# Room for two units of query weights, scalings on VectorE, spread splits and a later place for the value products

## The chip, the cores and the metric

The kernel runs on one core of one Trainium2 chip, as one program. The metric is device time in microseconds; the time before is the median of three runs, 2215.27 us (2212.75 to 2215.79). TensorE is called PE here, VectorE DVE, ScalarE ACT, GpSimd POOL, and SP is the engine that issues most DMA transfers.

## The reference

One inference step of an encoder with two layers, model width 1024, on 1024 prompt frames and 32 sample frames. Layer 0 is a recurrent mixer with a matrix memory (8 heads, chunks of 64), followed by a SwiGLU feed-forward part of width 2816. Layer 1 is windowed attention with 16 query heads and 2 shared key/value heads of 64, a learned sink per head and a linear distance bias, followed by another such feed-forward part. After each of the four parts the residual stream goes through `LayerNorm(alpha * x + part(x))`. The change lies in the attention:

```
q = x @ w_q;  k, v = split(x @ w_kv)
s = q k^T / 8 + bias                          # own chunk of 64 and the two chunks before
mx = max(max(s), sink)
p = exp(s - mx) / (sum exp(s - mx) + exp(sink - mx))
mix = (p v) @ w_out
x = LayerNorm(alpha * x + mix)
```

All values are 32-bit floats.

## The kernel before

**Numbers in two parts.** PE multiplies 32-bit floats of a rounded kind. Each operand is therefore split into a high part (a rounded copy) and a low part (operand minus high part), and each product is made of three matmuls: high by high, high by low, low by high. That is `gemm` (L416 to L418), in which nearly all matmuls of the program stand. Activations lie transposed, 128 features by 1056 columns for each of eight tiles k: `ACT` in full, `SX` as high and low part. Columns are cut into three groups (384, 384, 288) in the projections and into four quarters of 264 in the norms and the output projection.

**Weights.** The class `Weights` brings weights in units of 128 by 1024, in the fixed order in which they are used. A unit is loaded into one of four raw buffers (L168, on the SP queue; the load of a unit waits for the buffer of the unit four before) and split in two halves, or seven combinations for the feed-forward products. A split is a copy to the high part (L245 on ACT, or L243 on POOL for chosen halves) and a subtraction for the low part (L247, mostly on POOL). The results go to one of `SLOTS` = 5 slots. A half that has an entry in `W.home` goes to that place instead and needs no slot. `_next` makes the next split of the order or refuses: all slots in use, or the home still in use. Since the order is fixed, a refused half holds up all that follow it. `feed` calls it once per `W.pause` of issued matmul time; `done` frees the slots of a unit.

**Order of the work.** The program is written out as instruction streams, one per engine, each run in order. `Weave` mixes the work: side tasks are generators that yield how many microseconds of matmuls are to be issued before their next step, and each step of a `gemm` ticks them. So the order in which ACT, DVE and POOL get their work follows the matmuls of the issue order, not real time.

**From layer 0 to layer 1.** The last feed-forward products of layer 0 end with norms of the four quarters (`ln_task`, L477 to L531; DVE centres and scales, ACT squares, applies gain and bias and makes the high part at L525, DVE or POOL the low part at L531). While the last two norms run, the key unit and the value unit (`keys_values(0)`) and the first four query units (`q_group`, evacuated at L1686 by ACT and at L1689 by DVE) are multiplied for the first column group. Then the last norms are issued to their end, new PSUM pools are opened and the two score banks `psS` get columns cleared by DVE (L1752). The tasks `v_turn` (transposes the values, L1772, into `VR`) and `attention` are launched, and `keys_values(1)` and `keys_values(2)` follow with the next key unit and value unit. Until then the tiles for keys (`KH`, `KL`, two each of 1184 columns) beyond column 384 and for values (`VR`, 2560 columns) are allocated and empty.

**The attention** is a pipeline of six stages over items (head pair j, block b): `scores` (PE L1817, bias and maximum on DVE L1823), `soft` (ACT L1838), `scale` (reciprocal on DVE L1848, multiplication by it on POOL: L1851 for blocks of two chunks, L1855, one instruction per part, for the first and the last block), `turn` (PE transposes L1876, high part ACT L1880, low part DVE L1881), `values` (PE L1905, into the one bank `O`), `place` (ACT L1919 and DVE L1923 bring the result into `ACT`). A pass over the stages follows the last argument of `pipeline`, the tuple of stage numbers; a stage with a pause lets matmuls of the projections be issued before the next one.

**Splits of outputs.** The attention's output is split into `SX` for the output projection by `mixed_parts` (ACT L446, DVE or POOL L447), column group by column group and tile by tile: eight tiles k of a group need the query projections of that group to be done (`free`) and the tile's items to be placed (`mixed`). After each four tiles of the later groups, a DMA on SP brings the residual back (L1227). `nparts` counts finished groups and is what the output projection waits for. When the first quarter of the output projection is issued, `finish` issues what is left of the attention and of the splits at once.

Of the kernel before, what the change touches and what calls it, by code (L numbers as in the profile page):

```python
# [17 lines left out]
D = 1024  # L18
KT = D // P
# [12 lines left out]
EARLY = 3  # L32
# [18 lines left out]
FEED_W = 1.7  # L51
# [15 lines left out]
GRP = ((0, 384), (384, 384), (768, 288))  # L67
# [223 lines left out]
def kernel(ctx: ExitStack, tc: tile.TileContext, A, O):  # L291
    nc = tc.nc
# [61 lines left out]
    U_KV, U_QB, U_OUT_B = [], [[], []], [[], []]  # L354
# [857 lines left out]

    def mixed_parts(src, free, mixed, pauses, low=(nc.vector,)):


        for g in range(3):
            t0, n = GRP[g]
            while not free(g):
                yield 0.3
            for k in range(KT):  # L1220
                while not mixed(k, g):
                    yield 0.3
                split_act(k, g, low[k % len(low)])
                if g == 0:
                    nc.sync.dma_start(act[k][g], src[:, k, t0 : t0 + n])
                elif k % 4 == 3:
                    nc.sync.dma_start(act_g[g][:, k - 3 : k + 1], src[:, k - 3 : k + 1, t0 : t0 + n])  # L1227
                yield pauses[g]
            nparts[0] += 1

# [398 lines left out]
    home = [pb.tile([P, D // 2], F32R, name=f"oh{i}")[:] for i in range(2)]  # L1629
    W.home.update({(u, 1): home for u in U_QB[0][0:4:2] + U_OUT_B[0][:EARLY] + U_OUT_B[0][EARLY + 1 :: 2]})  # L1630
    vT = act[KT - 1]
# [95 lines left out]
    def keys_values(g):  # L1727
        if g == 2:
            k_part(ck[:], SEQ, P)
        for f, w in ((k_group, U_KV[g > 0][0]), (v_group, U_KV[g > 0][1])):  # L1730
            f(g)
            if g != 1:
                W.done(w)

    for t in tasks[:2]:
        wv.drain(t)
    keys_values(0)
    for j in range(4):
        q_group(j, 0)
        W.done(U_QB[0][j])  # L1740
    for t in tasks[2:]:
        wv.drain(t)
# [45 lines left out]
    def attention(gap):  # L1788
# [54 lines left out]
        def scale(j, b):  # L1843
# [5 lines left out]
            if 0 < b < 8:  # L1849
                w = p[:, 2 : 2 + 2 * WK].rearrange("p (c k) -> p c k", c=2)  # L1850
                nc.gpsimd.tensor_mul(w, w, st[:, 2].unsqueeze(2).broadcast_to([P, 2, WK]))  # L1851
            else:
                for c, _, at, nk, _, _ in parts(b):
                    w = p[:rows, at : at + nk]
                    nc.gpsimd.tensor_scalar_mul(w, w, st[:rows, 2, c : c + 1])  # L1855

# [50 lines left out]
        def place(j, b):  # L1907
# [28 lines left out]
            ],  # L1936
            (5, 3, 4, 2, 1, 0),
        )
# [28 lines left out]
    for n, (jp, g) in enumerate(JG):  # L1967
# [9 lines left out]
        if n == 3:  # L1977
# [5 lines left out]
                    lambda k, g: ast["placed"] >= last_item(k, g),  # L1983
                    (2.4, 1.0, 1.0),
                    (nc.vector, nc.gpsimd),
                )
            )
# [144 lines left out]
```

## Time and profile before

| | before |
|---|---|
| median of three runs | 2215.27 us (2212.75 to 2215.79) |
| the profiled execution, time | 2214.91 us |
| its span, first to last instruction | 2213.1 us |
| mean granted clock of PE | 0.996 |
| PE busy | 2170.9 us (98%) |
| DVE / ACT / POOL busy | 1435.8 / 990.1 / 986.5 us |
| DMA moved | 289.97 MB |

A view by stretches gives, for a stretch from A to B in microseconds from the span's start, its length, the busy time and number of instructions of PE, of its weight loads (PEld), of DVE, ACT and POOL, the clock that PE was granted as a share of full speed, the share of the DMA engines that was busy and what they moved. A view of waits gives who waited for whom, in total, how often, and the longest. A row of the timeline gives start, duration, engine, line, operation, output and inputs, shape, and in brackets how long the engine was idle before it and what released it. Rows that group instructions by shape give after the bar the busy time in us, the mean in ns and the idle time before them.

### The profile page before, as it was taken

The numbers are of one execution on the slowest core, as the hardware profiler recorded it, in microseconds if no ns is written. First come the engines' busy times: TensorE is split into PE (matmuls) and PEld (weight loads), VectorE is DVE, ScalarE is ACT, GpSimd is POOL, SyncE is SP. The second block draws the span as 40 slices with busy tenths as digits, with TensorE's granted clock in tenths as the row PEclk, the third lists the DMA queues.
The fourth block names the chain that finished last, engine by engine and source line by source line (L and its number), as shares of the span: only waits on it lengthen the run. The fifth ranks groups of instructions, "written<-read, shape, count | busy, mean of one in ns | idle before, by whom it ended". The sixth has DMA issues, their size and how long they took to land.

```text
span 2213.1 us, 43820 instructions
## 1 busy us (share of the span) xinstructions
PE 2170.9 (98%) x16982; PEld 2139.5 (97%) x16982; DVE 1435.8 (65%) x2794; ACT 990.1 (45%) x2229; POOL 986.5 (45%) x1010
## 2 busy tenths in 40 slices
PE   9999999999999999999998999899999999999997
PEld 9999999999999999999998989899999999999997
DVE  4465577787666665566667676788666656466657
ACT  4443455464444444322246676656444444432125
POOL 2544210004665555445515766700665556554441
PEclk9999999999999999999999999999999999999999
DMA  5222212212444343797514221321244334397712
GB/s 170 77 62 57 58 40 86 89 39 83 151 156 145 137 148 136 248 330 230 177 60 146 83 73 55 119 75 39 107 166 156 146 127 156 130 344 258 244 58 79
DMA packets 166192, 289.97 MB, mean 131 GB/s; under 512 B 16416, under 2 KB 121944, under 8 KB 165984
## 3 DMA queue, kind: packets, MB, share of 16 engines
q1 hardware_dynamic: 161632, 282.84, 38.4%
q10 hardware_dynamic: 4352, 4.33, 0.6%
q8 instruction: 134, 2.20, 0.4%
q14 instruction: 74, 0.61, 0.1%
HBM read 202.35 MB, written 82.94 MB: 129 GB/s over the span
## 4 chain that ended last, share of the span: by engine, by line
PE 84%; DVE 7%; ACT 4%; issue 2%; DMA 2%; POOL 1%; SPq 0%; POOLq 0%; DVEq 0%; ACTq 0%
PE d L416 10%; PE d L418 10%; PE d L417 10%; PE A L416 9%; PE A L417 9%; PE A L418 9%; PE B L416 7%; PE B L417 7%; PE B L418 7%; PE O L1905 1%; PE psS L1817 1%; ACT act L519 1%; DMA hs_x<-z 1%; DMA sx<-hs_t 1%; PE T L969 1%
## 5 line engine op out<-in xcount | busy, mean ns | idle before, releaser
L247 POOL TENSOR_TENSOR wl_s<-wr,wh_s 128x512 fp32r<-128x512 f32 x224 | 304.4, 1368 | 236.8 <-ACT wh_s L245 165.7
L416 PE MATMUL d<-sx,wh 128*128 128x264 f32 (+2 forms) x1052 | 337.8, 321 | 5.2 <-ACT wh L245 4.6
L247 POOL TENSOR_TENSOR wl_a<-wr,wh_a 128x512 fp32r<-128x512 f32 x112 | 153.3, 1371 | 402.0 <-ACT wh_a L245 397.5
L418 PE MATMUL d<-sx,wl 128*128 128x264 f32 (+2 forms) x1052 | 321.8, 306 | 2.4 <-POOL wl L247 2.3
L417 PE MATMUL d<-sx,wh 128*128 128x264 f32 (+2 forms) x1052 | 321.1, 305 | 0.4 <-DVE sx L447 0.4
L416 PE MATMUL A<-sx,wh_s 128*128 128x264 f32 x896 | 254.5, 284 | 0.5 <-ACT wh_b L245 0.5
L417 PE MATMUL A<-sx,wh_s 128*128 128x264 f32 x896 | 254.2, 284 | 0.0
L418 PE MATMUL A<-sx,wl_s 128*128 128x264 f32 x896 | 254.0, 284 | 0.0
L245 ACT CAST wh_s<-wr 128x512 fp32r<-128x512 f32 x224 | 135.7, 618 | 191.7 <-DVE wr L197 102.3
L416 PEld LDWEIGHTS d<-sx,wh 128*128 128x128 f32 x1052 | 199.6, 190 | 9.5 <-ACT wh L245 5.7
L418 PEld LDWEIGHTS d<-sx,wl 128*128 128x128 f32 x1052 | 198.7, 189 | 3.9 <-POOL wl L247 3.7
L417 PEld LDWEIGHTS d<-sx,wh 128*128 128x128 f32 x1052 | 199.7, 190 | 1.7 <-DVE sx L447 0.9
L416 PE MATMUL d<-sx,ex 128*128 128x264 f32 x624 | 180.7, 290 | 0.1
L418 PE MATMUL d<-sx,ex 128*128 128x264 f32 x624 | 177.0, 284 | 0.7 <-DVE ex L247 0.7
L417 PE MATMUL d<-sx,ex 128*128 128x264 f32 x624 | 177.2, 284 | 0.0
L416 PEld LDWEIGHTS A<-sx,wh_s 128*128 128x128 f32 x896 | 168.4, 188 | 0.7 <-ACT wh_b L245 0.7
L418 PEld LDWEIGHTS A<-sx,wl_s 128*128 128x128 f32 x896 | 168.8, 188 | 0.0
L417 PEld LDWEIGHTS A<-sx,wh_s 128*128 128x128 f32 x896 | 168.4, 188 | 0.0
L1343 POOL TENSOR_TENSOR z<-z 128x528 fp32r<-128x528 f32 x76 | 103.3, 1360 | 127.2 <-ACT z L1342 118.1
L247 POOL TENSOR_TENSOR wl<-wr,wh 128x512 fp32r<-128x512 f32 (+2 forms) x87 | 112.1, 1293 | 82.8 <-ACT wh L245 80.1
L416 PE MATMUL A<-ex,wh_s 128*128 128x264 f32 x448 | 127.5, 285 | 0.0
L417 PE MATMUL A<-ex,wh_s 128*128 128x264 f32 x448 | 127.1, 284 | 0.0
(361 smaller groups left out, 7183.4 us busy)
## 6 DMA issues: line engine op xcount, KB each, us to landing
wr<-in_gu SPq DMA_DIRECT2D x92, 512.0 KB, 4.5
hs_x<-z SPq DMA_DIRECT2D x72, 528.0 KB, 3.3
hs_t<-z SPq DMA_DIRECT2D x64, 528.0 KB, 2.7
sx<-hs_x SPq DMA_DIRECT2D x112, 264.0 KB, 6.0
sx<-hs_t SPq DMA_DIRECT2D x64, 264.0 KB, 6.2
ex<-hs_t SPq DMA_DIRECT2D x64, 264.0 KB, 6.3
wr<-in_dn SPq DMA_DIRECT2D x32, 512.0 KB, 4.5
ex<-hs_x SPq DMA_DIRECT2D x32, 264.0 KB, 6.4
```

The costliest lines, as they stand in the source:

```text
L245: self.nc.scalar.copy(hi, r)
L247: eng.tensor_sub(lo, r, hi.bitcast(F32))
L416: nc.tensor.matmul(out, ah, bh, start=start and k == 0, stop=False, **kw)
L417: nc.tensor.matmul(out, ah, bl, start=False, stop=False, **kw)
L418: nc.tensor.matmul(out, al, bh, start=False, stop=stop and k == last, **kw)
L519: nc.scalar.activation(z, z, AF.Identity, scale=gk, bias=bk)
L969: nc.tensor.matmul(pc[:, : 2 * (DV + 1)], keys, vt[j][:, c], start=True, stop=True)
L1343: eng.tensor_sub(lo.bitcast(F32R), buf(s), hi)
L1817: nc.tensor.matmul(ps[:rows, at : at + nk], lhs, k[:, k0 : k0 + nk], start=i == 0, stop=i == 1)
L1905: nc.tensor.matmul(out, v[:nk], x, start=i == 0, stop=i == len(todo) - 1)
```

## The change

1. *Room for weights.* The second and third query unit of the first four get homes for all four halves: the second in `VR` (four pieces of 512 columns), the third in columns 384 to 895 of `KH` and `KL`. The home `oh`, which the first and the third unit's second half shared, is now the first unit's only. While the first four query units are multiplied, `W.pause` is 1.3 instead of 1.7.
2. *Scalings.* The multiplications at L1855 go from POOL to DVE. Those at L1851 stay.
3. *Order in a pass.* `(5, 3, 4, 2, 1, 0)` becomes `(5, 3, 2, 1, 0, 4)`: `values` comes after `scale`, `soft` and `scores`.
4. *Splits.* `mixed_parts` takes a list of runs (group, tiles). For the attention it is: group 0 whole, then tiles 0 to 5 of group 1, tiles 0 to 5 of group 2, tiles 6 and 7 of group 1, tiles 6 and 7 of group 2, with pauses 2.4, 1.5, 1.5, 1.0, 1.0 instead of 2.4, 1.0, 1.0 by group. The other use of the function keeps its order.

```diff
-    def mixed_parts(src, free, mixed, pauses, low=(nc.vector,)):
-        for g in range(3):
+    WHOLE = [(g, range(KT)) for g in range(3)]
+
+    def mixed_parts(src, free, mixed, pauses, low=(nc.vector,), runs=WHOLE):
+        for (g, ks), pause in zip(runs, pauses):
             t0, n = GRP[g]
             while not free(g):
                 yield 0.3
-            for k in range(KT):
+            for k in ks:
...
-                yield pauses[g]
-            nparts[0] += 1
+                yield pause
+            if ks[-1] == KT - 1:
+                nparts[0] += 1
...
-    W.home.update({(u, 1): home for u in U_QB[0][0:4:2] + U_OUT_B[0][:EARLY] + U_OUT_B[0][EARLY + 1 :: 2]})
+    W.home.update({(u, 1): home for u in U_QB[0][:1] + U_OUT_B[0][:EARLY] + U_OUT_B[0][EARLY + 1 :: 2]})
+    flat = VR[:].rearrange("p c g a d -> p (c g a d)")
+    n = D // 2
+    spots = [flat[:, i * n : (i + 1) * n] for i in range(4)]
+    spots += [t[:, GRP[1][0] : GRP[1][0] + n] for t in (KH[0], KL[0], KH[1], KL[1])]
+    for i, u in enumerate(U_QB[0][1:3]):
+        for f in range(2):
+            W.home[u, f] = spots[4 * i + 2 * f : 4 * i + 2 * f + 2]
...
+    W.pause = 1.3
     for t in tasks[:2]:
         wv.drain(t)
     keys_values(0)
     for j in range(4):
         q_group(j, 0)
         W.done(U_QB[0][j])
+    W.pause = FEED_W
     for t in tasks[2:]:
         wv.drain(t)
...
-                    nc.gpsimd.tensor_scalar_mul(w, w, st[:rows, 2, c : c + 1])
+                    nc.vector.tensor_scalar_mul(w, w, st[:rows, 2, c : c + 1])
...
-            (5, 3, 4, 2, 1, 0),
+            (5, 3, 2, 1, 0, 4),
...
-                    (2.4, 1.0, 1.0),
+                    (2.4, 1.5, 1.5, 1.0, 1.0),
                     (nc.vector, nc.gpsimd),
+                    [WHOLE[0], *((g, ks) for ks in (range(6), range(6, KT)) for g in (1, 2))],
```

## The prediction, made before the changed kernel was run

> **What bounds the kernel now.** I read the page first, then the stretches around the step to the second layer, then the waits of PE there.
>
> ```profile
> span 2213.1 us, 43820 instructions
> PE 2170.9 (98%) x16982; PEld 2139.5 (97%) x16982; DVE 1435.8 (65%) x2794; ACT 990.1 (45%) x2229; POOL 986.5 (45%) x1010
> ```
>
> TensorE is busy for 2170.9 of 2213.1 us, so the program ends when its matmuls are through. The change takes away no matmul; it can only give back time in which PE waits or runs slowly. All of its edits act between 1166 us (first key product of layer 1) and 1440 us. Per stretch (length; busy time of PE, PEld, DVE, ACT, POOL; granted clock; DMA share; GB/s):
>
> ```profile
> 1183.00:1191.00 8.00, 8.00 (x47) 8.00 (x46) 5.40 (x7) 7.47 (x16) 4.19 (x4) 1.00 0.58 177
> 1191.00:1206.00 15.00, 9.30 (x36) 7.84 (x35) 11.60 (x15) 11.14 (x22) 8.23 (x8) 0.77 0.47 147
> 1206.00:1222.00 16.00, 13.14 (x80) 12.08 (x78) 8.52 (x52) 8.48 (x37) 10.71 (x20) 0.89 0.37 100
> 1222.00:1398.00 176.00, 170.53 (x1218) 160.60 (x1218) 120.47 (x481) 121.40 (x403) 120.73 (x170) 1.00 0.24 70
> 1398.00:1440.00 42.00, 35.42 (x273) 33.04 (x273) 31.99 (x86) 24.26 (x68) 31.47 (x34) 1.00 0.48 154
> ```
>
> In the first row PE is full: 47 matmuls in 8 us, 0.17 us each. In the second, 36 matmuls should take 6.1 us and take 15: 8.9 us are lost, partly by waiting, partly because the clock falls to 0.77. The waits of PE from 1190 to 1440 us (in total, times, longest):
>
> ```profile
> PE d L416 <- ACT wh L245: 4.6, 2, 4.1
> PE O L1905 <- DVE act L1923: 4.4, 4, 1.7
> PE T L1876 <- POOL s L1855: 2.9, 2, 2.6
> PE T L1876 <- POOL s L1851: 1.9, 2, 1.3
> PE d L418 <- POOL wl L247: 1.6, 3, 0.7
> PE O L1905 <- DVE lo L1881: 0.8, 2, 0.6
> PE d L418 <- DVE ex L247: 0.7, 1, 0.7
> ```
>
> Each of the four edits stands opposite some of these rows: weights (L245, L247), scalings (L1855), values (L1905), splits of outputs (they share DVE and POOL with the rest).
>
> **Part 1: query weights into empty room, pause 1.3.** Before, a half of a weight needs one of five slots or the one spare home. The last query unit and the first key unit of the next columns therefore get their casts late, and ScalarE is itself behind:
>
> ```profile
> 1191.53 0.62 ACT L245 CAST wh<-wr 128x512 fp32r<-128x512 f32 x1
> 1194.09 1.11 ACT L519 ACTIVATE act<-act,lnb,lng 128x264 f32<-128x264 f32 x2 [1.95 <-DVE act L511]
> 1199.05 0.61 ACT L245 CAST wh<-wr 128x512 fp32r<-128x512 f32 x1
> 1202.74 0.62 ACT L245 CAST wh<-wr 128x512 fp32r<-128x512 f32 x1
> 1203.39 0.98 ACT L1686 ACTIVATE Q<-d 64x384 fp32r<-64x384 f32 x2
> ```
>
> The cast at 1199.05 is the 4.1 us wait. With the change four halves go to the value and key tiles, so three fewer ask for a slot. By the order of issue the casts of the fourth query unit then stand some 8 to 9 us of matmul after the first key product, and that of the next key unit at about 11, instead of 16 and 18. The rows below say that data and GpSimd keep up: the first subtraction after the step is at 1172.33, the load of the next key unit follows it, and such a load lands in 4.1 us, by 1178. Six more subtractions of 1.29 us end at about 1181, ten before PE needs the last of them.
>
> ```profile
> 1172.33 1.29 POOL L247 TENSOR_TENSOR oh<-wr,oh 128x512 fp32r<-128x512 f32 x1
> 1173.65 0.35 SPq L168 DMA_DIRECT2D wr<-in_wkv  x1
> wr<-in_wqb SPq DMA_DIRECT2D x16, 512.0 KB, 4.1
> ```
>
> On the SP queue each load still waits for the subtraction that frees its buffer, with the copies of the keys behind it; these move some 2 us later and are needed only at the first scores, 30 us on. Key and value writes must now wait for the second and third query products; those end some 8 us before. So the weight wait goes. What is late next is the norm of the last quarter, which DVE and ACT still work off, and behind which stand the clearing of the score banks and the first scores:
>
> ```profile
> 1199.18 0.71 DVE L531 TENSOR_TENSOR sx<-act,sx 128x528 fp32r<-128x528 f32 x1 [0.82 <-ACT sx L525]
> 1203.89 1.39 DVE L531 TENSOR_TENSOR sx<-act,sx 128x528 fp32r<-128x528 f32 x1
> 1205.30 1.12 DVE L1689 SCALAR_TENSOR_TENSOR Q<-d,Q 64x384 fp32r<-64x384 f32 x2
> 1206.49 0.62 DVE L1752 MEMSET psS<- 128x1 f32 x6
> 1207.74 0.19 PE L1817 MATMUL psS<-KH,Q 128*128 128x64 f32 x1
> ```
>
> Without the weight wait the fourth query product ends near 1193.6 (half a unit, 12 matmuls of 0.17, from 1191.5) and the key product follows at once; the attention is issued 4.0 us of matmul later, so PE reaches the first score near 1198 and then waits for the memset. That memset comes earlier only by what leaves the queues in front of it: two casts (1199.05 and 1202.74) of 0.62 us, 1.2 us; and 0.7 us if the last L531 takes 0.71 instead of 1.39 because POOL is then idle. So the first score moves from 1207.74 to about 1205.8: **1.9 us**, not 8.9. The upper bound is 8.9 (nothing else is late), the lower is -2: a longer unbroken wait than the present 4.1 us could hold the half clock longer, and in the second row the low clock already costs 15 x 0.23 = 3.5.
>
> **Part 2: small scalings on VectorE.** 24 instructions leave POOL.
>
> ```profile
> 1213.26 0.41 POOL L1714 COPY bt<-nsink 64x4 f32<-64x4 f32 x2 [2.12 <-DMA bt<-in_bias]
> 1214.43 2.03 POOL L1855 TENSOR_SCALAR s<-s,st 128x64 f32<-128x64 f32 x4
> L1855 POOL TENSOR_SCALAR s<-s,st 64x160 f32<-64x160 f32 x8 | 5.4, 680 | 7.4 <-ACT t L1919 4.1 <-DVE st L1848 3.4
> L1855 POOL TENSOR_SCALAR s<-s,st 128x128 f32<-128x128 f32 x8 | 4.8, 606 | 0.0
> L1855 POOL TENSOR_SCALAR s<-s,st 128x64 f32<-128x64 f32 x8 | 3.9, 484 | 0.4
> L1104 DVE TENSOR_SCALAR sg<-sg 128x384 f32<-128x384 f32 x12 | 4.2, 352 | 0.0
> L1001 DVE TENSOR_SCALAR small<-small 128x2 f32<-128x2 f32 x32 | 7.1, 223 | 23.6 <-ACT junk L994 23.6
> ```
>
> The first scalings stand behind a copy that waits 2.12 us for a bias table; on DVE they follow the reciprocal at once and wait for nothing that it hasn't waited for. The 2.9 us of PE go, and with them the slow clock after it: 16 x 0.11 = 1.8 us. Sum 4.7; I take **4.2**, the rest for the first products that then lean on POOL's next scaling. Price: DVE has no row of this shape; by the two nearest one costs 0.22 to 0.35 us, 24 of them 5.3 to 8.4 us, beside 176 us in which DVE is busy 120.5. Behind each stand the next score reductions and low parts. Bounds: 0 (POOL's L1851 is late instead) to 4.7.
>
> By the Trainium skill (TensorE: Matmul & The Clock Gate, "What's actually happening") the clock halves after about 3.4 us of idling; by that the 2.6 us wait costs no clock and this part gives 2.9. The row differs (0.89 behind that wait), so the measurement stands.
>
> **Part 3: values later in a pass.** DVE's and ACT's order stays as it is; only PE issues scores and one 0.46 us step of matmuls before the value products. So the output bank (L1923) and the low parts (L1881) have about 0.9 us more. The rows hold 4.4 + 0.8 us; the longest single one, 1.7, belongs to part 4. Of the other 3.5, in pieces of 1.7 at most, I take **2.5**. Bounds: -1 (the next scores press on their bank) to 3.5.
>
> **Part 4: splits of outputs spread.** Six of the eight splits of the last columns move ahead of the last two of the middle columns.
>
> ```profile
> 1420.53 2.60 DVE L447 TENSOR_TENSOR sx<-act,sx 128x288 fp32r<-128x288 f32 x1
> 1420.58 1.27 POOL L247 TENSOR_TENSOR wl<-wr,wh 128x512 fp32r<-128x512 f32 x1
> 1421.82 1.00 POOL L447 TENSOR_TENSOR sx<-act,sx 128x384 fp32r<-128x384 f32 x1
> 1424.10 0.36 PE L1905 MATMUL O<-hi,VR 128*128 128x256 f32 x1 [1.71 <-DVE act L1923]
> 1428.15 0.46 DVE L447 TENSOR_TENSOR sx<-act,sx 128x288 fp32r<-128x288 f32 x1
> 1428.66 1.77 ACT L446 CAST sx<-act 128x288 fp32r<-128x288 f32 x5
> ```
>
> The DVE split of 2.60 us holds up the addition that frees the bank: 1.7 us of PE. Five splits in a row at 1428.66 press POOL and DVE where PE then waits 0.7 for L247. With the change two remain there and the long one is past by then. I take **1.7**; bounds -2 (the same splits now hit passes from 1400 to 1410) to 2.4. Their SP copies move with them and nothing waits for those.
>
> **Sum.** 1.9 + 4.2 + 2.5 + 1.7 = 10.3. Below that I put 1.3 back, because a freed PE meets POOL scalings (1.9 us of L1851 now) sooner: 9. The profiled execution took 2214.9 us around its span of 2213.1; less 9 is 2205.9. It lies 0.4 under the median of the three runs, 2215.27, so I forecast **2206**.
>
> **Rivals.**
> 1. *The norm isn't in the way*: the early casts also shorten the exchange between ACT and DVE from 1182 on, and most of 8.9 comes back. For it: ACT and DVE wait for each other there (1.95 at 1194.09). Against: the casts fill gaps in which ACT waits anyway. Then 7 more: 2199.
> 2. *The change moves waits only*, or the new room comes free too late, so that the casts stay where they were: the memset stays at 1206.5, POOL's L1851 takes over L1855's wait. Parts 3 and 4 alone, halved by a fuller DVE: 2 us, 2213. For it: in the last two stretches DVE, ACT and POOL are each 58 to 76% busy, so latencies, not one engine, pace the attention.
> 3. *Slower: DVE and POOL shut each other out.* The 2.60 us split covers exactly the two POOL instructions above (1420.58 to 1422.8); a split of the same shape at 1428.15 takes 0.46. If each of the 24 scalings so waits for a POOL subtraction or scaling, say 1.1 us, DVE loses 26 us in front of low parts and reductions; it decides once about half of that reaches PE: 13 - 6 from the rest, 2222. Against: the reciprocal in the same place shows no such wait, and POOL itself loses 5.4 + 4.8 + 3.9 = 14 us of work.
> The Trainium skill (SBUF — State Buffer, "SBUF: two separate sides") says that the pair of ports shared by these two engines is locked for a whole instruction and the other blocks; the 2.60 us row agrees.
>
> **How the numbers follow.** Forecast (gains of 5 to 13) 0.57; rival 1 0.14; rival 2 0.19; rival 3 0.10. Faster by over 0.2% (4.4 us, about what can be told from no change): 0.57 + 0.14 = 0.71; within: 0.19; slower: 0.10. The sum by its lowest bounds is -5, by its highest 19.5; not all fall together. Range 2198 to 2216: it holds the forecast, rival 2 and most of rival 1, and leaves out rival 3.
>
> **What would show it.** Part 1: no wait on L245 from 1190 to 1206, instead one of the first score or of a bank on DVE, first score near 1205.8; if it comes before 1203, rival 1. If L245's 4.6 us stay, the room came late. Part 2: L1855 on DVE at 0.2 to 0.4 us each and no wait on it; above 0.8 mean, rival 3. Part 3: L1905's waits on L1923 and L1881 under 2 us. Part 4: at most two splits in the last batch, no DVE split over 1.5 us there. The forecast is wrong if PE's loss outside 1190 to 1440 us changes, since nothing there is touched.

## The result, and the profile after

The changed kernel took 2206.36 us (median of 6 runs, 2203.71 to 2207.24), the kernel before 2212.95 us (6 runs beside it, 2212.07 to 2215.79): a ratio of 0.9966, 95% interval 0.9953 to 0.9979. That is 6.6 us less by the medians and 7.5 us by the ratio, with an interval of 4.6 to 10.4. The runs of the kernel before lie in two groups (four at 2212.07 to 2213.03 us, two at 2215.27 and 2215.79), so that differences of its medians are rough and the ratio decides wherever the two differ. The forecast of 2206 us is met; the terms that made it up are not, as the rest shows.

The head of the page of the changed kernel:

```profile
span 2205.4 us, 43768 instructions
PE 2168.4 (98%) x16982; PEld 2141.5 (97%) x16982; DVE 1445.6 (66%) x2818; ACT 990.7 (45%) x2229; POOL 976.1 (44%) x986
```

The matmuls are the same 16982. The 24 scalings have gone from POOL (1010 to 986 instructions) to DVE (2794 to 2818). The span is 7.7 us shorter. Not all of that is the change's: the first key product of layer 1, up to which both kernels do the same, started at 1166.93 us before and starts at 1165.90 now. So 1.0 us was gained ahead of the first edit, and some 6.7 us behind it.

The changed kernel by stretches (length; busy time of PE, PEld, DVE, ACT, POOL; granted clock; DMA share; GB/s):

```profile
1191.00:1206.00 15.00, 8.62 (x40) 7.98 (x39) 11.42 (x20) 11.22 (x24) 5.60 (x5) 0.86 0.46 138
1206.00:1222.00 16.00, 16.00 (x97) 15.47 (x98) 10.61 (x59) 9.37 (x41) 6.74 (x15) 0.81 0.21 52
1222.00:1398.00 176.00, 170.25 (x1236) 162.14 (x1236) 130.64 (x516) 123.97 (x410) 117.47 (x159) 1.00 0.25 73
1398.00:1440.00 42.00, 38.55 (x293) 37.06 (x293) 33.77 (x75) 24.85 (x63) 22.81 (x24) 0.96 0.56 190
```

The first row still loses 8.2 of its 15 us (40 matmuls of 0.17 us each; with 36 matmuls it lost 8.9), and the second row is "busy" for all of its 16 us only because the clock stands at 0.81 there: a matmul at half clock counts as busy for twice as long. The granted clock is 1.00 or 0.50 at any moment in the clock records of these traces, so a stretch of length L with mean clock c holds 2(1 - c)L of half clock: 4.2 and 6.1 us in these two rows, 10.3 in all, as much as before (6.9 and 3.5). The half clock moved; it didn't go.

The waits of PE in the changed kernel, from 1170 to 1440 us (in total, times, longest):

```profile
PE psS L1829 <- issue: 4.1, 1, 4.1
PE T L1888 <- POOL s L1863: 4.0, 2, 2.5
PE d L416 <- DVE Q L1699: 2.2, 1, 2.2
PE psS L1829 <- DVE st L1835: 1.8, 3, 1.1
PE O L1917 <- DVE act L1935: 0.8, 1, 0.8
...
PE O L1917 <- ACT hi L1892: 0.5, 1, 0.5
```

Lines have moved: the scores are L1829, the transposes L1888, the value products L1917, the additions that free their bank L1935, POOL's scalings of two chunks L1863, DVE's small ones L1867. Each of the rows that the prediction opposed to an edit is gone or smaller: the weight wait on L245 (4.6), the wait on the small scalings (2.9), the waits of the value products (4.4 and 0.8, now 0.8, and 0.5 on ACT's high part). In their place stand a wait of the first score (4.1), of a bank that DVE frees at L1699 (2.2), and of POOL's large scalings (1.9 before, 4.0 now).

**Where the time went.** For each matmul we took the time to the start of the next one, less its columns at 0.457 ns each (the median from start to start is 121 ns for 264 columns and 175 ns for 384) or 0.106 us, whichever is more, and summed this over three stages, counted from the first key product so that the offset of 1 us drops out: *start*, 20 to 55 us after it (weights, first scores, first scalings); *passes*, 55 to 225 us; *end*, 225 to 275 us. In us lost: start 14.5 before and 11.9 after, passes 17.1 and 13.5, end 10.7 and 9.8. The gains are 2.6, 3.6 and 0.9, together 7.1. Outside these stages PE lost 37.4 + 0.8 and 13.4 us before, 36.3 + 0.8 and 13.6 after.

### The profile page after: what moved, and what is told of

Its sections match the earlier page's. It is cut to its first block, busy times and chain, and to the rows that moved or that the text cites. A ratio compares the mean times of both kernels' runs of the same rounds, so it can differ in the third digit from the quotient of the medians.

```text
span 2205.4 us, 43768 instructions
## 1 busy us (share of the span) xinstructions
PE 2168.4 (98%) x16982; PEld 2141.5 (97%) x16982; DVE 1445.6 (66%) x2818; ACT 990.7 (45%) x2229; POOL 976.1 (44%) x986
## 4 chain that ended last, share of the span: by engine, by line
PE 88%; DVE 6%; ACT 3%; issue 1%; DMA 1%; POOL 1%; SPq 0%; ACTq 0%; DVEq 0%; POOLq 0%
PE d L416 10%; PE d L418 10%; PE d L417 10%; PE A L416 10%; PE A L418 10%; PE A L417 10%; PE B L416 7%; PE B L417 7%; PE B L418 7%; PE O L1917 1%; PE psS L1829 1%; PE T L1888 1%; ACT act L519 1%; DMA hs_x<-z 1%; PE T L969 1%
## 5 line engine op out<-in xcount | busy, mean ns | idle before, releaser
L247 POOL TENSOR_TENSOR wl_s<-wr,wh_s 128x512 fp32r<-128x512 f32 x224 | 304.3, 1368 | 237.4 <-ACT wh_s L245 168.9
L416 PE MATMUL d<-sx,wh 128*128 128x264 f32 (+2 forms) x1040 | 333.5, 321 | 2.9 <-DVE Q L1699 2.2
L247 POOL TENSOR_TENSOR wl_a<-wr,wh_a 128x512 fp32r<-128x512 f32 x112 | 153.2, 1371 | 402.2 <-ACT wh_a L245 396.9
L417 PE MATMUL d<-sx,wh 128*128 128x264 f32 (+2 forms) x1040 | 316.9, 305 | 0.4 <-DVE sx L447 0.4
L245 ACT CAST wh_s<-wr 128x512 fp32r<-128x512 f32 x224 | 135.9, 619 | 192.4 <-DVE wr L197 102.8
L416 PEld LDWEIGHTS d<-sx,wh 128*128 128x128 f32 x1040 | 197.0, 189 | 6.6 <-ACT act L519 2.5
L417 PEld LDWEIGHTS d<-sx,wh 128*128 128x128 f32 x1040 | 197.3, 190 | 1.5 <-DVE sx L447 0.7
L247 POOL TENSOR_TENSOR wl<-wr,wh 128x512 fp32r<-128x512 f32 (+2 forms) x84 | 108.9, 1302 | 85.6 <-ACT wh L245 82.8
```

What stands on the lines that cost most here:

```text
L245: self.nc.scalar.copy(hi, r)
L247: eng.tensor_sub(lo, r, hi.bitcast(F32))
L416: nc.tensor.matmul(out, ah, bh, start=start and k == 0, stop=False, **kw)
L417: nc.tensor.matmul(out, ah, bl, start=False, stop=False, **kw)
```

## The experiments

Each kernel is compared with the kernel before, run beside it on the same chip. The table is worked out from the traces as above; half clock is 2(1 - c)L over the rows 1191 to 1206 and 1206 to 1222 of each. The losses are those of one profiled execution per kernel, and the stages vary between executions: `p3_values` and `p4_splits` change nothing that the start depends on by its place in the program, and lose 11.2 and 15.3 us there where the kernel before lost 14.5. In `low_parts_on_dve` 2.0 us more are lost ahead of the stage *start* (2.8 instead of 0.8 us), so its 10.9 doesn't compare with the other rows.

```
kernel                 ratio to before, interval    lost: start passes end   half clock in the start
before                 1                                  14.5   17.1  10.7   10.4
after                  0.9966 [0.9953, 0.9979]            11.9   13.5   9.8   10.3
p1_room                0.9989 [0.9980, 0.9998]            10.7   17.4  10.3    6.8
p2_scaling             0.9988 [0.9979, 0.9997]            10.0   18.9   9.5    6.9
p3_values              0.9963 [0.9951, 0.9976]            11.2   12.7   9.3    6.9
p4_splits              0.9997 [0.9988, 1.0006]            15.3   16.5  10.3   13.6
p13_room_values        0.9956 [0.9943, 0.9968]            12.0   12.7   9.4   10.0
p23_scaling_values     0.9954 [0.9941, 0.9966]            10.1   13.8   9.4    6.9
p123_no_splits         0.9960 [0.9947, 0.9972]            12.3   12.7   9.7   10.0
late_attention         0.9974 [0.9965, 0.9983]            10.9   15.1   9.8    3.5
clear_on_act           0.9972 [0.9961, 0.9982]            12.6   12.7  10.3   10.0
low_parts_on_dve       0.9978 [0.9969, 0.9987]            10.9   12.8  10.5    6.8
casts_off_pool         0.9945 [0.9932, 0.9957]            11.5   13.9   4.3    6.9
best_without_room      0.9930 [0.9917, 0.9944]            10.6   13.7   3.9    6.9
```

### Each part alone

**p1_room**: the kernel before with part 1 only (the homes in `VR`, `KH`, `KL`, and the pause of 1.3).

```diff
-    W.home.update({(u, 1): home for u in U_QB[0][0:4:2] + U_OUT_B[0][:EARLY] + U_OUT_B[0][EARLY + 1 :: 2]})
+    W.home.update({(u, 1): home for u in U_QB[0][:1] + U_OUT_B[0][:EARLY] + U_OUT_B[0][EARLY + 1 :: 2]})
...
+    for i, u in enumerate(U_QB[0][1:3]):
+        for f in range(2):
+            W.home[u, f] = spots[4 * i + 2 * f : 4 * i + 2 * f + 2]
...
+    W.pause = 1.3
```

> Part 1 alone (homes in the value and key tiles, pause 1.3). Theory of the prediction: only the first score moves, by 1.9 us; the 2.9 us wait on the POOL scaling stays, so the time falls by about 2. Theory from the trace after: POOL, freed of the late subtractions, also reaches the first scalings sooner, so part 1 alone already takes away most of the wait on L1855, and the time falls by 2.5 to 4; DVE's norm (L486 to L511 around 1176 to 1184 us) shows the 4 us of longer instructions that the changed kernel shows, because the early subtractions run beside it.

2210.92 us against 2215.38; by the ratio 2.4 us less, with an interval of 0.4 to 4.4. Two waits of PE in it, from 1170 to 1440 us:

```profile
PE psS L1826 <- issue: 4.1, 1, 4.1
PE d L416 <- DVE Q L1696: 2.2, 1, 2.2
```

The weight wait (4.6 on L245) is gone and two waits take its place, 4.1 + 2.2: by waits alone the part gives nothing there. Yet the start loses 3.8 us less. The gain lies elsewhere: no wait on the small scalings is left, though they still run on POOL. The bias table shows why. The transfer's issue on the SP queue before (POOL's copy after it, at 1213.26 with 2.12 us of idling, stands in the prediction), then POOL's copy and the issue with part 1:

```profile
1207.53 0.43 SPq L1710 DMA_DIRECT2D bt<-in_bias  x1
```

```profile
1207.61 0.41 POOL L1721 COPY bt<-nsink 64x4 f32<-64x4 f32 x2
1195.37 0.43 SPq L1717 DMA_DIRECT2D bt<-in_bias  x1
```

On the SP queue the table's transfer stands behind the weights' loads, and each of those waits for its buffer. With room for the weights the table is issued 10.5 us sooner, counted from the first key product (30.1 us after it instead of 40.6), POOL's copy finds it there, and the 2.12 us of idling in front of the scalings go. POOL itself also comes to this copy sooner: the copy starts 42.4 us after the first key product instead of 46.3, and 1.9 of these 4.0 us are subtractions of weights (L247) that no longer stand in front of it. Part 1 so takes away the very wait that the prediction gave to part 2. The norm's five instructions on DVE take 8.0 us here, as in the changed kernel.

**p2_scaling**: the one line that puts the small scalings on DVE.

```diff
-                    nc.gpsimd.tensor_scalar_mul(w, w, st[:rows, 2, c : c + 1])
+                    nc.vector.tensor_scalar_mul(w, w, st[:rows, 2, c : c + 1])
```

> Part 2 alone (L1855 on DVE). Theory of the prediction: the wait of 2.9 us and the half clock behind it go, 4.2 us faster, the weight wait of 4.6 us and the first score at 1207.7 stay. If parts 1 and 2 take away the same wait, this run gains as much by itself (3.5 to 4.7), and the sum of the gains of parts 1 and 2 is well over what both give together. Rival (DVE and POOL shut each other out): not faster, DVE scalings of 0.8 us and more.

2211.05 us against 2215.38; by the ratio 2.7 us less, with an interval of 0.7 to 4.6. The stretch in which the first scalings lie, and one of the waits that are left, in this kernel:

```profile
1206.00:1222.00 16.00, 16.00 (x120) 15.32 (x119) 12.38 (x66) 10.92 (x48) 10.32 (x20) 1.00 0.35 97
```

```profile
PE O L1905 <- DVE lo L1881: 1.7, 3, 0.9
```

120 matmuls lie where 80 lay, at clock 1.00 instead of 0.89: the wait of 2.6 us and the half clock behind it are gone, and the start loses 4.5 us less (4.2 predicted). In the passes it is given back in part: 18.9 against 17.1, with PE's waits for the low parts (L1881) at 1.7 instead of 0.8 us and those of its weight loads from 1222 to 1398 us at 6.0 instead of 4.9. So 24 more instructions on DVE cost some 1.8 us there in this execution.

**p3_values**: the order of a pass.

```diff
-            (5, 3, 4, 2, 1, 0),
+            (5, 3, 2, 1, 0, 4),
```

> Part 3 alone (values last in a pass). Prediction: 2.5 us. Theory from the trace after: 4 us, all between 1222 and 1400 us, with the waits of L1905 on L1923 and L1881 down from 5.2 to about 1. Rival: 0, because the waits move to the next scores (psS on DVE L1823), which would then show 3 us and more.

2205.45 us against 2215.38; by the ratio 8.2 us less, with an interval of 5.3 to 10.8, as much as the whole change. The passes in this kernel, the same stretch in p1_room, and the wait of the value products that is left in this kernel:

```profile
1222.00:1398.00 176.00, 171.45 (x1252) 163.86 (x1251) 124.77 (x498) 125.69 (x414) 130.00 (x179) 1.00 0.27 80
```

```profile
1222.00:1398.00 176.00, 168.81 (x1203) 158.47 (x1202) 121.77 (x482) 122.75 (x405) 123.87 (x172) 1.00 0.26 77
```

```profile
PE O L1905 <- DVE act L1923: 3.4, 3, 1.5
```

p1_room has the old order and comes into this stretch at nearly the same point of its work (first key product at 1165.26 in both, 0.5 us apart in what the start loses); it does 1203 matmuls there, this kernel 1252. The loss in the passes falls by 4.4 us, in the end by 1.4. The waits of L1905 that PE's own list names fall from 5.2 to 3.4 us only, where about 1 was expected: from 3.2 to 1.5 at the end, from 2.0 to 1.8 in the passes. The passes' gain shows in the waits of the weight loads (PEld), which PE's list doesn't hold. From 1222 to 1398 us, before and with part 3:

```profile
PEld O L1905 <- DVE lo L1881: 4.9, 13, 0.8
PEld O L1905 <- DVE lo L1881: 1.7, 5, 0.3
```

By the sum over matmuls of above, PE lost 6.2 us of the passes just ahead of the products with the low parts before, and 2.6 with part 3. So the mechanism is the one that was meant: the low parts have more time. It is not one execution's luck, for all ten kernels of the table with part 3 lose 12.7 to 15.1 us in the passes, and the four without it 16.5 to 18.9.

The start fell by 3.3 us too. The edit has no place there. The bias table was issued 40.6 us after the first key product in both kernels, but POOL could copy it 4.0 us after the issue here and 5.7 before, so that POOL idled 0.34 instead of 2.12 us for it. Why the transfer took less isn't shown: in the two other kernels with part 3 and without part 1 the copy came 5.3 and 4.3 us after the issue, in the three with neither 5.7 to 5.8. So 5.8 us belong to the edit as the stages show it, and the 3.3 at the start stay open.

**p4_splits**: the runs of the splits.

```diff
-                    (2.4, 1.0, 1.0),
+                    (2.4, 1.5, 1.5, 1.0, 1.0),
                     (nc.vector, nc.gpsimd),
+                    [WHOLE[0], *((g, ks) for ks in (range(6), range(6, KT)) for g in (1, 2))],
```

> Part 4 alone (order and pauses of the output splits). Prediction: 1.7 us, and no DVE split over 1.5 us behind 1398 us. Theory from the trace after: at most 0.5 us, because the splits that moved forward meet POOL full of weight casts, and the wait of the transposes on POOL's L1851 grows from 1.9 to about 4 us as it did in the changed kernel.

2214.30 us against 2215.38: no difference that can be told. Its waits:

```profile
PE T L1879 <- POOL s L1854: 3.4, 2, 2.2
PE O L1908 <- DVE act L1926: 1.2, 2, 1.0
```

The wait of the value products falls from 4.4 to 1.2, as meant; the wait on POOL's large scalings rises from 1.9 to 3.4. One replaced the other, and the end gained 0.4 us.

### Parts together

**p13_room_values**, **p23_scaling_values** and **p123_no_splits** are the parts of their names together, with the edits above.

> Parts 1 and 3 together, scalings and splits as before. If the four parts act on different waits, the gain is that of part 3 alone (0.37%, about 8 us) and that of part 1 alone (0.11%, 2.4 us) together, 10 us. If they overlap (all of the first scalings' wait on POOL is gone with either), 8 to 9 us. If the room costs as much on DVE (the norm beside the early subtractions) as it gives, 8 or less.

> Parts 2 and 3 together. Different waits: 8 and 2.7 us, 10 to 11. Theory that the scalings on DVE take back in the passes what they give at the first scalings: 6 to 8 us, with waits of the scores' bank on DVE L1823 over 1.5 us where part 3 alone has 0.6.

> Parts 1, 2 and 3, splits as before. If part 4 is worth nothing, as it was alone, this equals the changed kernel (0.34%, 6.6 us to 7.5 us). If part 4 costs something beside the others (POOL scalings late at the end, 4.0 us in the changed kernel), 8 us and more; if it gives what was predicted (1.7 us), 5 to 6 us.

2205.57, 2205.19 and 2206.20 us against 2215.36. The intervals overlap, so the times alone don't rank them. The traces say more of the start. With neither part 1 nor part 2 it loses 14.5, 11.2 and 15.3 us (before, p3_values, p4_splits); with part 2 of the two 10.0, 10.1 and 10.6 (p2_scaling, p23_scaling_values, best_without_room); with part 1 of the two 10.7 and 12.0 (p1_room, p13_room_values); with both 11.9, 12.3 and 11.5 (the changed kernel, p123_no_splits, casts_off_pool). So part 2 takes some us off, part 1 does so less surely (its 12.0 lies over the 11.2 of p3_values), and both together take no more than part 2 alone. With part 2 done, part 1 doesn't add: in these traces it takes 1 to 2 us away. The half clock in the start is 10.0 us in both kernels with room here and 6.9 in the one without; half of the 3.1 us more is 1.6, most of the difference of 2.2. The whole change against p123_no_splits shows part 4 once more: end 9.8 and 9.7, with 0.8 instead of 3.0 us of waits of the value products on DVE's additions and 4.0 instead of 2.1 on POOL's large scalings. By the ratios p123_no_splits gains 8.9 us and the whole change 7.5; the intervals overlap, so a cost of part 4 isn't shown.

### What the first score waits for

**late_attention**: p13_room_values, with the attention issued 4 us of matmul later, so that PE has the next weights' products to do while the norm ends.

```diff
-        yield 4.0
+        yield 8.0
-    wv.launch(v_turn(0, 3.0))
+    wv.launch(v_turn(0, 7.0))
```

> Parts 1 and 3, and the attention is issued 4 us of matmul later (8.0 and 7.0 in place of 4.0 and 3.0). Theory that the first score waits for DVE's clearing of its bank behind the norm: the 4.1 us wait in front of the first score goes, a wait of about 2 us for a bank of the second key product on DVE L1689 comes in its place, and the time falls by 1.5 to 2.5 us against parts 1 and 3 alone. Rival (PE waits for something else there, or the attention's length decides): the wait stays 4 us, or the time rises by up to 4 us because the attention ends later.

2209.00 us against 2215.36. The stretch of the weight and score waits in this kernel, and its waits:

```profile
1191.00:1206.00 15.00, 11.21 (x64) 10.63 (x63) 11.42 (x20) 11.46 (x25) 5.55 (x5) 1.00 0.41 128
```

```profile
PE T L1885 <- POOL s L1864: 4.6, 4, 2.6
PE T L1885 <- POOL s L1860: 3.7, 3, 1.6
PE psS L1826 <- issue: 1.6, 1, 1.6
```

64 matmuls instead of 46 (p13_room_values in the same stretch) and no half clock there: the work to cover the wait was there, and the first score's wait fell from 4.1 to 1.6 us. But PE waited on POOL's scalings, 4.6 + 3.7 us, and the start lost 10.9 against 12.0, the passes 15.1 against 12.7. POOL's copies of the bias tables show where most of these waits come from:

```profile
1213.58 0.41 POOL L1721 COPY bt<-nsink 64x4 f32<-64x4 f32 x2 [5.20 <-DMA bt<-in_bias]
1230.11 0.41 POOL L1721 COPY bt<-nsink 64x4 f32<-64x4 f32 x2 [7.53 <-DMA bt<-in_bias]
```

The attention's issue brings the table's transfer with it. Issued later, the transfer stands behind copies of the keys on the SP queue: it went out at 1210.79 us here and at 1197.01 in p13_room_values, where POOL waited for neither table. Three waits of PE, 5.6 of the 8.3 us, follow these two copies. So the edit moved more than it was meant to, and the run doesn't show what covering the first score's wait alone would give.

**clear_on_act**: the changed kernel with the clearing of the score banks on ACT.

```diff
-            nc.vector.memset(t[:, c : c + 1], 0.0)
+            nc.scalar.activation(t[:, c : c + 1], eps_ln[:], AF.Copy, scale=0.0)
```

> The changed kernel, with the columns of the score banks cleared by ScalarE (a copy scaled by zero) instead of DVE. Theory that the first score waits for the clearing, which stands behind the norm in DVE's queue: the wait in front of the first score falls from 4.1 us to 1.5 to 2.5, because ScalarE is through with the last query copy near 1203.5 where DVE clears at 1205.6 to 1206.2, and the half clock behind it gets shorter or goes; 1 to 3 us less in this stretch. Rival (PE waits there for the queries' low parts or for the bank of the second key product): the wait stays at 4 us.

2207.46 us against 2213.91, not better than the change. The first score's wait now has a name, and the clearing in front of it too (a wait, then a row of the timeline of this kernel):

```profile
PE psS L1829 <- ACT psS L1764: 4.3, 1, 4.3
```

```profile
1206.47 1.09 ACT L1764 ACTIVATE psS<-eps_ln 128x1 f32<-128x1 f32 x6 [2.04 <-DVE Q L1699]
```

So "issue" in the row of the changed kernel stood for the clearing: the first score does wait for it, as predicted. But the wait stayed at 4.3 us where 1.5 to 2.5 was expected: ACT, free, waited 2.04 us itself for DVE's last step on the queries (L1699, their low parts). So it wasn't the order on DVE alone that held the clearing up: the banks are released by DVE's work on the queries, and the rival that named their low parts was right in that.

**low_parts_on_dve**: the changed kernel with the low parts of three query units on DVE instead of POOL.

```diff
+    on_vector.update((u, f) for u in U_QB[0][1:4] for f in range(2))
```

> The changed kernel, with the low parts of the second to fourth query unit on DVE instead of POOL (six subtractions). Theory that in the changed kernel the early subtractions on POOL stretch the norm's instructions on DVE (L486, L489 and L511 from 1176 to 1184 us take 8.0 us there, 3.9 in the kernel before): they go back to 4 to 5 us in all, while the six subtractions cost DVE 6 x 0.69 = 4.1, so that the first score comes within 1 us of where it is in the changed kernel. Rival (the norm is stretched by something else, ACT or the DMA): the 8 us stay, and the first score comes 4 us later.

2208.69 us against 2213.91. In the changed kernel the norm runs beside POOL's early subtractions, and is slow. DVE before, DVE after and POOL after, from their timelines (start, us, instruction):

```profile
1177.12 2.14 DVE L486 TENSOR_TENSOR z<-z 128x528 f32<-128x528 f32 x2
1179.30 0.43 DVE L489 TENSOR_TENSOR z<-z 128x264 f32<-128x264 f32 x1
1179.65 1.32 DVE L511 TENSOR_TENSOR act<-act,z 128x528 f32<-128x528 f32 x2
```

```profile
1176.11 3.06 DVE L486 TENSOR_TENSOR z<-z 128x528 f32<-128x528 f32 x2
1179.21 1.40 DVE L489 TENSOR_TENSOR z<-z 128x264 f32<-128x264 f32 x1
1180.53 3.51 DVE L511 TENSOR_TENSOR act<-act,z 128x528 f32<-128x528 f32 x2
1175.11 3.50 POOL L247 TENSOR_TENSOR KL<-wr,KH 128x512 fp32r<-128x512 f32 x2
1178.57 4.91 POOL L247 TENSOR_TENSOR wl<-wr,wh 128x512 fp32r<-128x512 f32 x3
```

The same five instructions take 3.9 us before and 8.0 after, and POOL's subtractions 1.75 and 1.64 us each where 1.29 was their time before. With the low parts on DVE:

```profile
1182.37 0.72 DVE L490 TENSOR_TENSOR z<-z 128x264 f32<-128x264 f32 x1
1183.02 2.39 DVE L512 TENSOR_TENSOR act<-act,z 128x528 f32<-128x528 f32 x2
```

The last three of the five fall from 4.9 to 3.1 us and all five from 8.0 to 5.6 (4 to 5 expected), but the subtractions now stand in DVE's own queue (0.69 us each), the first score starts 2.3 us later counted from the first key product (within 1 expected), and PE waits 1.8 us for the norm's sums (z, L490), which it didn't before. In these rows the two engines hold each other up; taking one out of the other's way by giving it the work doesn't pay.

### The end, and a version that beats both

**casts_off_pool**: the changed kernel, with the high parts of the first output weights on ACT instead of POOL.

```diff
-    on_gpsimd.update((u, f) for u in U_QB[1] + U_OUT_B[0] for f in range(2))
+    on_gpsimd.update((u, f) for u in U_QB[1] for f in range(2))
```

> The changed kernel, with the high parts of the first output weights copied by ACT instead of POOL. Theory that at the end of the attention POOL, full of weight splits, is what the transposes wait for: the wait on L1863 (4.0 us, two times) falls under 1.5 and the time by 1.5 to 3 us. Rival (the splits that part 4 moved forward hold POOL, or ACT becomes late in turn): that wait stays over 3 us, or waits on ACT (L1892, L245) of 2 us and more come up, and the time stays within 1 us.

2200.98 us against 2213.91. In the changed kernel the wait on POOL's large scalings at the end had this in front of it, on POOL:

```profile
1406.71 0.85 POOL L243 CAST wh<-wr 128x512 fp32r<-128x512 f32 x1
1407.64 1.26 POOL L247 TENSOR_TENSOR wl<-wr,wh 128x512 fp32r<-128x512 f32 x1
1408.86 1.61 POOL L1863 TENSOR_TENSOR s<-s,st 128x384 f32<-128x384 f32 x2
```

The last stretch of casts_off_pool:

```profile
1398.00:1440.00 42.00, 40.96 (x326) 39.48 (x325) 35.90 (x82) 26.68 (x65) 17.98 (x17) 1.00 0.58 187
```

326 matmuls instead of 293, clock 1.00 instead of 0.96, no wait on L1863 in the list any more (4.0 in the changed kernel), and the end loses 4.3 us instead of 9.8. Some 1.7 of these 5.5 us are half clock, of which the changed kernel has a period of 3.4 us from 1410.16, behind the longer of its two waits. By the ratios this edit gives 4.6 us, over the 1.5 to 3 expected. So it is shown that POOL, busy with casts of weights, was late with the large scalings at the end. That the casts also took part 4's gain is argued: no run has them on ACT without part 4.

**best_without_room**: casts_off_pool without part 1.

```diff
-    W.home.update({(u, 1): home for u in U_QB[0][:1] + U_OUT_B[0][:EARLY] + U_OUT_B[0][EARLY + 1 :: 2]})
...
-            W.home[u, f] = spots[4 * i + 2 * f : 4 * i + 2 * f + 2]
+    W.home.update({(u, 1): home for u in U_QB[0][0:4:2] + U_OUT_B[0][:EARLY] + U_OUT_B[0][EARLY + 1 :: 2]})
...
-    W.pause = 1.3
```

> Parts 2, 3 and 4 of the change and the first output weights' high parts on ScalarE as in casts_off_pool, but without part 1: the query weights keep their old places and the old pause. Theory (the room costs more than it gives once the scalings no longer wait): the wait on ScalarE's high part of the query weight (4 to 5 us) is back, and still the loss up to the first score and its scalings falls from about 11.5 us in casts_off_pool to about 10, since GpSimd's early subtractions no longer stretch the norm and there is one period of half clock of 6.8 us; ratio to the kernel before 0.993 to 0.994, below casts_off_pool's 0.9945. Rival (the room gives what it takes, or its gain is the larger now): ratio 0.9945 to 0.996. In both the end of the attention keeps its loss of 4 to 5 us and shows no wait on GpSimd's large scaling above 1 us.

2199.43 us against 2214.98: the fastest kernel of the study, 15.5 us under the kernel before. The stretch of its first scores and scalings, and its longest wait:

```profile
1206.00:1222.00 16.00, 16.00 (x119) 15.35 (x118) 11.79 (x66) 10.79 (x46) 9.65 (x20) 1.00 0.35 97
```

```profile
PE d L416 <- ACT wh L245: 4.6, 2, 4.1
```

The first scalings run at full clock, 119 matmuls where the changed kernel has 97. The weight wait of 4.6 us is back, and the start still loses no more than with the room (10.6 against 11.5; end 3.9 against 4.3). The two ratios' intervals overlap (0.9917 to 0.9944 and 0.9932 to 0.9957), so that part 1 costs time isn't shown by the times; but in neither pair of kernels with and without it (casts_off_pool and this one, p123_no_splits and p23_scaling_values) does it give any, once the scalings are on DVE.

## Why the prediction was right, and which of its terms were not

**Total.** 9 us were forecast; the gain is 6.6 us by the medians and 7.5 by the ratio. That the time still came out at 2206 is luck in the starting point: the forecast set out from 2215.27, the median of three runs, and with three runs more that median is 2212.95, 2.3 us lower. In the profiled executions the gain is 7.7 us, of which 6.7 came from the change and 1.0 from code that it doesn't touch. The forecast said it would be wrong if the loss outside 1190 to 1440 us changed; it changed by 1.1 us ahead of it. The first key product starts between 1165.26 and 1167.63 us in the fourteen kernels of the table, with nearly the same code in front of it, so a single profiled execution carries about 1 us either way that no edit explains.

**Part 1 (1.9 predicted).** The signs came as named: no wait on L245, instead a wait of the first score and one of a bank that DVE frees, and the first score at 1206.0 (1205.8 predicted). Three rows of the changed kernel, DVE's then PE's:

```profile
1203.66 0.71 DVE L531 TENSOR_TENSOR sx<-act,sx 128x528 fp32r<-128x528 f32 x1
1205.58 0.62 DVE L1764 MEMSET psS<- 128x1 f32 x6
1206.00 0.39 PE L1829 MATMUL psS<-KH,Q 128*128 128x64 f32 x1 [4.14 <-issue]
```

L531 did shorten to 0.71. But the match of the first score is luck. Counted from the first key product, the clearing stands at 39.6 us before (1206.49 - 1166.93) and at 39.7 after (1205.58 - 1165.90): it didn't move. The step that failed is "That memset comes earlier only by what leaves the queues in front of it": the early subtractions, which the prediction let run on POOL for nothing, stretched the norm from 3.9 to 8.0 us and took back what left the queues. The last norm's first L531 starts 32.0 us after the first key product instead of 30.7, 1.3 late; the cast that no longer stands at 1199.05 gave back 0.5, the shorter L531 0.7, and the cast at 1202.74 nothing, since DVE was busy then. best_without_room has the norm at 3.9 us again and its clearing at 39.5. The first score itself came 0.7 us sooner, from 40.8 to 40.1. What part 1 did give it gave in a place that the prediction costed at nothing: POOL's first scalings, for which the bias table's transfer came 10.4 us sooner past the weights on the SP queue and POOL's late subtractions were out of the way. The prediction looked on that queue at the key copies only.

**Part 2 (4.2 predicted).** Alone it gave 4.5 us at the start against the profiled execution before, half clock included, so the size was right for it alone; how much of the wait other executions have isn't shown (p3_values, with neither part, loses 3.3 less). The sum was wrong: it added parts 1 and 2, and both take away the same wait. 6.1 was predicted for the start, 2.6 came (2.2 without part 4). And the price on DVE, hidden in the prediction beside 176 us with DVE busy for 120.5, isn't all hidden: 1.8 us of the passes in p2_scaling, 1.1 in p23_scaling_values against p3_values, but none in p123_no_splits against p13_room_values. All scalings of the changed kernel on DVE (durations least, median, most, in ns):

```profile
L1867 DVE TENSOR_SCALAR s<-s,st x24: 255/290/1291, 1209.7 to 1413.5; 128x64 f32<-128x64 f32 x8, 128x128 f32<-128x128 f32 x8, 64x160 f32<-64x160 f32 x8
```

The estimate of 0.22 to 0.35 us from two other shapes held for the median, 0.29.

**Part 3 (2.5 predicted, at most 3.5).** Too small: 4.4 us in the passes and 1.4 at the end. The mechanism was right. The step that failed took its gain from the waits that PE's own list names (3.5 us). Those hardly moved in the passes (2.0 to 1.8 us); what moved is the wait of the weight loads for the low parts, 4.9 to 1.7, which the prediction didn't look at. The count of matmuls in the passes shows the same (1252 against 1203). In the whole change the passes gained 3.6. The waits on L1923 and L1881 fell from 5.2 to 0.8 with all parts, under the 2 us named.

**Part 4 (1.7 predicted).** Nothing that can be measured alone, and end 9.8 against 9.7 with it and without it among the others. The splits on DVE in the last stretch of the changed kernel:

```profile
L447 DVE TENSOR_TENSOR sx<-act,sx x5: 459/989/1155, 1400.1 to 1422.2; 128x288 fp32r<-128x288 f32 x4, 128x384 fp32r<-128x384 f32 x1
```

None is over 1.5 us, as named, and the 1.7 us wait on L1923 went. The last batch holds four splits, not two at most. In the place of the gain came the wait on POOL's large scalings, 4.0 us instead of 1.9. The prediction had put 1.3 us back for just this, by a guess over the whole sum; it was about the whole of part 4.

**Rivals.** Rival 1 (the norm isn't in the way) fell: the first score waits 4.1 us with its weights there. Rival 2 (waits only move) was right about the end and about the weight wait, though not about the total. Rival 3's cause is there, in the norm (3.9 to 8.0 us) and in the scaling of 1291 ns (at 1413.51, beside a subtraction on POOL that starts at 1413.41 and takes 1287 ns), at a few places and not at each scaling; the median of 290 ns decides against its 1.1 us. The rule that the prediction quoted from the Trainium skill (SBUF — State Buffer, "SBUF: two separate sides"), that a VectorE instruction with two inputs in SBUF and a GpSimd one lock each other out, fits these rows: the stretched norm instructions and the subtractions both read two operands from SBUF, and both got longer.

So the total was right since errors cancelled. In gains, by stage: the start 6.1 predicted, 2.6 measured; the passes 2.5 and 3.6; the end 1.7 and 0.9; less the 1.3 put back, 9.0 against 7.1. The wait counted twice at the start (3.5 too much) and the end (0.8) were offset in part by the 1.3 and by the passes (1.1). What was left over, 2.4 us by the medians (9 against 6.6), the lower starting point made good.

## What to carry to other kernels

Two edits that each free a different resource can remove the same wait: before adding their gains, ask for each wait which of the edits alone would already end it, transfers that move up in a shared queue included. When an edit brings work on one engine forward "for nothing", look at what the other engines do at that time: here the subtractions on POOL stretched the norm on DVE from 3.9 to 8.0 us. Read the waits of the weight loads beside those of the matmuls: the largest gain of this change stood there. Where a removed wait was replaced by one on the next engine, as at the end here, the gain came once other work left that engine (9.8 us lost against 4.3). And look for luck in the starting point before calling a forecast good: its baseline moved by 2.3 us with three more runs.

## What was not expected of the hardware

The clock's fall isn't set by the length of a wait alone. The same wait of 2.2 us, at the same place, is followed by half clock in one kernel and not in another. PE's timeline of the changed kernel, where the stretch from 1191 to 1206 us had the clock 0.86 and the first score waited 4.14 us until 1206.00:

```profile
1195.13 0.66 PE L416 MATMUL d<-sx,wh 128*128 128x384 f32 x1 [2.24 <-DVE Q L1699]
```

The same stretch of casts_off_pool, and the two waits in its timeline:

```profile
1191.00:1206.00 15.00, 7.20 (x41) 6.52 (x39) 11.42 (x20) 11.25 (x24) 5.56 (x5) 0.95 0.45 138
```

```profile
1195.18 0.41 PE L416 MATMUL d<-sx,wh 128*128 128x384 f32 x1 [2.20 <-DVE Q L1699]
1206.04 0.39 PE L1829 MATMUL psS<-KH,Q 128*128 128x64 f32 x1 [5.64 <-issue]
```

In the first, half clock began at 1195.12 us by the trace's clock records and lasted 3.4 us; in the second it didn't come until 1204.6. Half-clock periods came in lengths of 3.4 or 6.8 us in all fourteen kernels, but for the last of each execution, which runs into its end. These two rows also show what that period was worth: the second kernel did its products at full clock, was done 1.5 us earlier, and waited 1.5 us longer (5.64 against 4.14) for the same first score at 1206.0. In this pair half clock cost nothing, since PE was not what the first score waited for. The Trainium skill (TensorE: Matmul & The Clock Gate, "What's actually happening") has a free-running window of 3.4 us decide on the clock; the steps of 3.4 us agree with that, and chance in where a wait falls in such a window would explain the pair, but no run here moved a wait against it to show so. Why kernels with room get 3.4, 6.8 or 10 us of half clock at the start stays open for the same reason.
